# A two-block sequence model on one core: the recurrence's elementwise part moved from its eight units of 128 tokens into the projections, by pairs of heads and halves of the tokens

## The chip, the cores and the metric

The kernel runs as one program on one core of a Trainium2 chip. The metric is the device time of one execution in microseconds (us), the median of several runs. The engines are called PE (TensorE, matrix products), DVE (VectorE), ACT (ScalarE), POOL (GpSimd) and SP (SyncE, which here only issues DMAs). Each engine takes its own instructions in a fixed order and waits for the others by semaphores.

## The reference

Two blocks over 1024 tokens (16 more in the first) of width 1024, in float32. The first block (a state-space branch, an mLSTM branch and a gated FFN) is not touched. The second block normalizes, projects, and runs two mixers side by side: an 8-head recurrence (RWKV-7, 64 wide) and an 8-head dilated attention. An output product and an FFN follow. The part that the change moves is the recurrence:

```python
def _rwkv7_scan(r, decay, k, v, kk, a):
    def step(state, inp):
        r_t, w_t, k_t, v_t, kk_t, a_t = inp
        sa = jnp.einsum('bhvk,bhk->bhv', state, -kk_t)
        state = (state * w_t[:, :, None, :]
                 + sa[..., None] * (kk_t * a_t)[:, :, None, :]
                 + v_t[..., None] * k_t[:, :, None, :])
        return state, jnp.einsum('bhvk,bhk->bhv', state, r_t)
...
    p = p + (_token_shift(p) - p) * shift_mix
    w_log = -jax.nn.softplus(-(w0 + jnp.tanh(wd) @ w_lora_up)) - 0.5
    decay = jnp.exp(-jnp.exp(w_log.astype(f32)))
    a = jax.nn.sigmoid(a0 + ad @ a_lora_up)
    kk = heads(k * k_k)
    kk = kk / jnp.maximum(jnp.sqrt(jnp.sum(kk * kk, axis=-1, keepdims=True)), 1e-12)
    k = k * (1.0 + (a - 1.0) * k_a)
...
    bonus = jnp.sum(rh * kh * r_k.astype(f32), axis=-1, keepdims=True) * vh
```

The kernel computes the scan in chunks of 32 tokens: in a chunk a triangular system is solved, which turns the 32 steps into small matrices; a chain of products then carries the state from chunk to chunk.

## The kernel before

A scheduler with a model of the engines lays out each engine's instructions when the program is built, so the order on an engine is fixed, and an instruction whose input is late holds up all that stand behind it on that engine. Tiles live in pools by tag, with a number of buffers each: `W` 6, `V` 4, `A` and `L` 3, `J`, `B`, `K` 2, and `U`, which holds the matrix `M` of the triangular system, 1.

Around the change the second block runs these stages:

- **`rkv`** (L1333): twelve projections by `shifted` (L1297), for k, then r, then v, four groups of 128 columns each. A group is 48 products of 128x512 (three per 128 rows of the input, for float32 accuracy), in two halves of 512 tokens; here a **chunk** is one half, 24 products. DVE copies a half out (`p<-pm,rs`), POOL takes the difference of neighbouring tokens (`d`), DVE mixes. ACT and DVE split each weight tile into a high and a low part (`whi`, `wlo`). Groups of k go through `removal` (L1354: scaling, norm over a head). All results go to DRAM (`drkv`).
- **`rwkv`** (L1532): eight units u0 to u7 of 128 tokens. `rwkv_unit` (L1373) loads four tiles of 128x4x128 (partitions x head pairs x tokens) from `drkv`, through ACT's DMA queue, computes the decay by small products (`pa<-sl,lw`, L1390), tanh, a running sum (L1395) and exponentials, then about twenty elementwise operations. The operands go to `products` (L1429), whose first result is masked into `MM`. `MM` goes to DRAM (`dm`) and comes back as `M`, arranged for POOL. The **solve** is 31 steps of two POOL instructions (`fs<-Z,M`, `Z<-Z,fs`). Its result goes to DRAM (`dz`) and comes back as `xt`. All of these transfers go through SP.
- **`rwkv_maps`** (L1470) makes four 96x96 maps per head from `xt`, one unit later, and **`rwkv_chain`** (L1515) carries the state through them, two units later.
- **`attn_in`** (L1617): 24 chunks of projections for the attention, whose products the scheduler lays between those of the recurrence.
- The attention itself, whose products are ordered by hand; its first comes after the last products of the recurrence's chain.

`M` has one buffer, so a unit's `M` is loaded only when the solve before has ended.

Of the kernel before, what the change touches and what calls it, by code (L numbers as in the profile page):

```python
# [48 lines left out]
class Build:  # L49
# [1211 lines left out]
    def lora_weights(self):  # L1261

        self.reset = self.small([P, P], tag="reset", bufs=1)
        self.nc.gpsimd.memset(self.reset, 1.0)
        self.nc.gpsimd.memset(self.reset[:, 0:P:32], 0.0)
# [53 lines left out]
    def lora_part(self, part):  # L1319

        nc = self.nc
        raw = self.small([64, NT], tag="lrw", bufs=1)
        self.dma(out=raw, in_=self.dlora[:64, NT * part:NT * part + NT])
        sl = self.small([96, 2, NT], F32R, tag="sl", bufs=1)
# [8 lines left out]
    def rkv(self):  # L1333
# [4 lines left out]
        for i in (1, 0, 2):  # L1338
            for j in range(4):
# [6 lines left out]
                for h in range(2):  # L1346
                    ps = self.bank([P, 4, P], "c1")
                    for k in range(4):
                        self.nc.tensor.transpose(ps[:, k], t[:, 512 * h + 128 * k:512 * h + 128 * k + 128], self.ident)
                    vn = t[:, 512 * h:512 * h + 512].rearrange("p (k v) -> p k v", v=P)  # L1350
                    self.nc.scalar.copy(vn, ps)
                    self.dma(out=self.dvn[512 * h:512 * h + 512, j].rearrange("(k t) v -> t k v", t=P), in_=vn)

# [19 lines left out]
    def rwkv_unit(self, u, sl):  # L1373

        nc, v, pool, par = self.nc, self.nc.vector, self.nc.gpsimd, self.par
        t0 = P * u
        ch = lambda t: t.rearrange("p q (c t) -> p q c t", t=32)
        tw, ta, kk = (self.slot([P, 4, P], name="pr", tag="W") for _ in range(3))
        cs, rn, K, V = (self.slot([P, 4, P], name="pr", tag="V") for _ in range(4))
        R = self.slot([P, 4, P], name="R", tag="K")  # L1380
        wd = self.small([64, 4, 4, 2], tag="wd", bufs=4)
        cols = lambda n: [(par[n] if isinstance(n, str) else n)[:, q:q + 1] for q in range(4)]
        for i, t in ((3, kk), (0, R), (1, K), (2, V)):
            self.store(out=t, in_=self.drkv[i, :, :, t0:t0 + P].rearrange("q p t -> p q t"))

        own = slice(P * (u % 2), P * (u % 2) + P)
        for q in range(4):
            ps = self.bank([P, 2, NT], "a")
            for i in range(2):
                nc.tensor.matmul(ps[:, i], self.lw[:, i, q * P:q * P + P], sl[:, i], start=True, stop=True)  # L1390
            self.act(tw[:, q], ps[:, 0, own], AF.Tanh, scale=0.5, bias=self.w0h[:, q:q + 1])
            self.act(ta[:, q], ps[:, 1, own], AF.Tanh, scale=0.5, bias=self.a0h[:, q:q + 1])
        self.ts(tw, tw, 1.0, ALU.add)
        for q in range(4):
            v.tensor_tensor_scan(out=cs[:, q], data0=self.reset, data1=tw[:, q], initial=0.0, op0=ALU.mult, op1=ALU.add)  # L1395
        rate = -0.5 * math.exp(-0.5)
        W, WI = tw, cs
        self.act(tw, cs, AF.Exp, scale=rate)
        self.act(cs, cs, AF.Exp, scale=-rate)
        for e in range(2):  # L1400
            v.tensor_copy(wd[:, :, :, e], ch(W)[64 * e:64 * e + 64, :, :, 31])

        for q, (a, b) in enumerate(zip(cols(self.ka1), cols(self.ka0))):
            self.ts(rn[:, q], ta[:, q], a, ALU.mult, b, ALU.add)
        self.stt(ta, ta, 1.0, kk, ALU.add, ALU.mult)
        self.tt(ta, ta, WI, ALU.mult)
        self.tt(ch(kk)[:, :, :, 1:], ch(kk)[:, :, :, 1:], ch(W)[:, :, :, :31], ALU.mult)
# [761 lines left out]
```

## Time and profile before

| | |
|---|---|
| time, median of 3 runs | 3239.7 us (3235.3 to 3243.54) |
| profiled execution | 3233.1 us, its span 3231.4 us |
| busy in the span | PE 3009.3 us (93%), DVE 2009.6 (62%), POOL 1335.0 (41%), ACT 1142.4 (35%) |
| chain that ended last | PE 61%, DVE 11%, POOL 7%, issue 5%, DMA 4% |
| moved by DMA | 336.83 MB, mean 104 GB/s |

The span runs from the first to the last instruction of the profiled execution. The chain is followed back from the end, at each step to what released the instruction. Shares of a whole span average over stages with different limits, so the rows further down are cut to stages: `rkv` from 1642.7 to 1796.5 us, the eight solves from 1831.9 to 2150.0 us, the last products of the chain at about 2194 us.

### The profile page before, as it was taken

How to read it: one execution, taken by the hardware profiler on the slowest of the kernel's cores; microseconds unless marked ns; L12 is line 12 of the kernel's file. 1: busy time of each engine (PE TensorE's matmuls, PEld its weight loads, DVE VectorE, ACT ScalarE, POOL GpSimd, SP SyncE). 2: the span in 40 equal slices, each digit the busy share in tenths (PEclk: the TensorE clock that was granted, in tenths of full speed). 3: DMA queues.
4: the chain of work that ended last, by engine and by line, in shares of the span. 5: the costliest groups of instructions: out<-in, count | busy, mean ns of one | idle time of the engine just before them, and what ended most of it. 6: DMA issues, size and time to landing. Idle time of an engine off the chain costs nothing.

```text
span 3231.4 us, 52682 instructions
## 1 busy us (share of the span) xinstructions
PE 3009.3 (93%) x20614; PEld 2678.5 (83%) x20614; DVE 2009.6 (62%) x3618; ACT 1142.4 (35%) x2168; POOL 1335.0 (41%) x1291
## 2 busy tenths in 40 slices
PE   7999999989799999999999988788988899999998
PEld 6999998979799999877877776677778788887777
DVE  7556654674676666466776555558656766664666
ACT  3344313334343333311333323424444333334111
POOL 3767310033654444232532365543214744454430
PEclk9999999989799999999899989858998899999999
DMA  5333532335222222432223554533425122224321
GB/s 148 86 94 111 174 98 59 105 101 139 78 66 79 81 82 81 150 104 74 90 95 131 146 126 112 137 99 108 115 98 196 53 85 79 80 83 174 113 85 53
DMA packets 322535, 336.83 MB, mean 104 GB/s; under 512 B 60081, under 2 KB 270734, under 8 KB 322286
## 3 DMA queue, kind: packets, MB, share of 16 engines
q1 hardware_dynamic: 289646, 310.38, 31.0%
q10 hardware_dynamic: 32640, 23.08, 2.3%
q8 instruction: 162, 2.65, 0.3%
q14 instruction: 87, 0.71, 0.1%
HBM read 232.66 MB, written 96.40 MB: 102 GB/s over the span
## 4 chain that ended last, share of the span: by engine, by line
PE 61%; DVE 11%; POOL 7%; issue 5%; DMA 4%; ACT 2%; SPq 2%; ACTq 0%; DVEq 0%; POOLq 0%
PE pm L196 13%; PE pm L197 12%; PE pm L198 12%; PE px L197 5%; PE px L196 5%; PE px L198 5%; POOL fs L149 2%; POOL Z L149 2%; DVE dn L149 2%; SPq L142 2%; PE px L292 1%; DVE t L149 1%; PE pa L1877 1%; DMA M<-dm 1%; PE pc L1604 1%
## 5 line engine op out<-in xcount | busy, mean ns | idle before, releaser
L196 PE MATMUL pm<-xh,whi 128*128 128x512 f32 (+5 forms) x1344 | 446.9, 333 | 14.2 <-DVE th L149 11.5
L198 PE MATMUL pm<-xh,wlo 128*128 128x512 f32 (+5 forms) x1344 | 446.8, 333 | 0.0
L197 PE MATMUL pm<-xl,whi 128*128 128x512 f32 (+5 forms) x1344 | 446.4, 332 | 0.0
L149 DVE TENSOR_TENSOR y<-y,pm 128x512 f32<-128x512 f32 (+1 forms) x336 | 218.1, 659 | 159.4 <-PE pm L198 159.1
L196 PE MATMUL pm<-dn,dn 128*128 128x512 f32 (+1 forms) x736 | 286.0, 389 | 6.5 <-DVE y L149 6.2
L196 PEld LDWEIGHTS pm<-xh,whi 128*128 128x128 f32 (+1 forms) x1344 | 257.8, 192 | 35.8 <-DVE th L149 12.4
L197 PE MATMUL pm<-dn,dn 128*128 128x512 f32 (+1 forms) x736 | 282.4, 384 | 1.3 <-POOL dn L149 1.3
L198 PE MATMUL pm<-dn,dn 128*128 128x512 f32 (+1 forms) x736 | 282.5, 384 | 0.0
L197 PEld LDWEIGHTS pm<-xl,whi 128*128 128x128 f32 (+1 forms) x1344 | 257.6, 192 | 19.7 <-issue 0.9
L198 PEld LDWEIGHTS pm<-xh,wlo 128*128 128x128 f32 (+1 forms) x1344 | 257.8, 192 | 19.1 <-issue 0.5
L149 POOL TENSOR_TENSOR dn<-hid,dn 128x1024 fp32r<-128x1024 f32 x44 | 131.8, 3012 | 250.9 <-ACT dn L1161 250.9
L197 PE MATMUL px<-t,sh 128*128 128x258 f32 (+2 forms) x684 | 218.7, 320 | 6.9 <-DVE t L149 6.8
L196 PE MATMUL px<-t,sh 128*128 128x258 f32 (+2 forms) x684 | 217.2, 318 | 0.4 <-DVE gt L149 0.3
L198 PE MATMUL px<-t,sl 128*128 128x258 f32 (+2 forms) x684 | 216.1, 316 | 0.0
L149 DVE TENSOR_TENSOR wlo<-wraw,whi 128x1024 fp32r<-128x1024 f32 (+2 forms) x114 | 153.9, 1351 | 76.2 <-ACT whi L170 74.7
L196 PEld LDWEIGHTS pm<-dn,dn 128*128 128x128 f32 x736 | 138.2, 188 | 43.7 <-DVE y L149 14.2
L170 ACT CAST whi<-wraw 128x1024 fp32r<-128x1024 f32 (+2 forms) x114 | 103.4, 908 | 185.7 <-PE pm L197 154.8
L197 PEld LDWEIGHTS pm<-dn,dn 128*128 128x128 f32 x736 | 138.4, 188 | 29.9 <-POOL dn L149 1.7
L198 PEld LDWEIGHTS pm<-dn,dn 128*128 128x128 f32 x736 | 138.2, 188 | 30.0
L170 ACT CAST dn<-wd 128x1024 fp32r<-128x1024 f32 x44 | 46.1, 1048 | 290.8 <-PE pm L197 290.3
L197 PEld LDWEIGHTS px<-t,sh 128*128 128x128 f32 x684 | 131.3, 192 | 17.9 <-DVE t L149 9.1
L149 POOL TENSOR_TENSOR wraw<-wraw,par 128x1024 f32<-128x1024 f32 (+1 forms) x36 | 73.4, 2041 | 169.0 <-DMA wraw<-in_w_in_dram 128.7
(600 smaller groups left out, 8788.6 us busy)
## 6 DMA issues: line engine op xcount, KB each, us to landing
wraw<-in_w_in_dram SPq DMA_DIRECT2D x61, 512.0 KB
dhid<-up SPq DMA_DIRECT2D x44, 512.0 KB
wd<-in_w_ffn_down_dram SPq DMA_DIRECT2D x44, 512.0 KB
hid<-dhid SPq DMA_DIRECT2D x44, 512.0 KB
wra<-in_w_ffn_up_dram SPq DMA_DIRECT2D x33, 512.0 KB
wrb<-in_w_ffn_up_dram SPq DMA_DIRECT2D x33, 512.0 KB
dg<-th SPq DMA_DIRECT2D x16, 514.0 KB
wraw<-in_w_out_dram SPq DMA_DIRECT2D x16, 512.0 KB
```

The source lines that it names most:

```text
L142: self.nc.sync.dma_start(out=out, in_=in_)
L149: (eng or self.nc.vector).tensor_tensor(out=o, in0=a, in1=b, op=op)
L170: self.nc.scalar.copy(hi, src)
L196: nc.tensor.matmul(ps, a[0], b[0], start=start, stop=False, **kw)
L197: nc.tensor.matmul(ps, a[0], b[1], start=False, stop=False, **kw)
L198: nc.tensor.matmul(ps, a[1], b[0], start=False, stop=stop, **kw)
L292: self.nc.tensor.matmul(ps[:bw, i:i + 1], src[:, i * bw:i * bw + bw], self.ones[:, 0:1], start=start and i == 0, stop=stop and i == n - 1)
L1604: nc.tensor.matmul(ps, w[:, k], (yh, yl, yh)[q][:, a:b], start=i == 0, stop=i == 11)
L1877: nc.tensor.matmul(self.po[:, i - 4 * ch], pT[:, i * P - a:i * P - a + P], self.vx[j % 2][:, k].rearrange("p e v -> p (e v)")[:, 2 * e:2 * ...
```

## The change

The elementwise part of `rwkv_unit` becomes a function of its own, `prepare(q, half)`, called eight times from `rkv`: for each pair of heads q (one group of 128 columns) and each half of 512 tokens, on tiles of 128x512. `rkv` now takes k, v and r of one group in turn, then that group's two `prepare`s. A `prepare` loads its four tiles from `drkv`, and stores four results to a new DRAM tensor `dprep` and the bonus to `dbon`, all through SP. A unit then only loads its four tiles from `dprep`, through SP, and starts with `products`. It needs one half's `prepare` of all four pairs, so u0 needs that of the last pair. The transposed copy of v gets a buffer of its own (`B`) instead of overwriting its source. `MM` gets its own buffer in `W`. One tile holds the decays at the ends of all chunks (`wd`).

Instructions, before to after: decay products 64 of 256 columns to 16 of 512; tanh 64 of 128x128 to 16 of 128x512; running sums, scalings by `k_a` and multiplications by `r_k` each 32 of 128x128 to 8 of 128x512; 40 DMA issues leave ACT (32 loads, 8 stores of the bonus); SP gets 32 loads of `drkv`, 32 stores and 32 loads of `dprep` and 8 stores of the bonus (256 KB each). POOL's instructions stay the same in number.

```diff
     def rkv(self):
...
-        for i in (1, 0, 2):
-            for j in range(4):
+        self.dprep = self.dram([4, 4, P, T2], "dprep")
+        self.wd = self.small([64, 4, 32, 2], tag="wd", bufs=1)
+        sl = [self.lora_part(h) for h in range(2)]
+        for j in range(4):
+            for i in (1, 2, 0):
                 t = self.shifted(512 * i + j * P, P, self.par["mix"][:, 4 * i + j:4 * i + j + 1])
                 self.dma(out=self.drkv[i, j], in_=t)
...
-                    vn = t[:, 512 * h:512 * h + 512].rearrange("p (k v) -> p k v", v=P)
+                    vn = self.slot([P, 4, P], name="vn", tag="B")
...
+            for h in range(2):
+                self.prepare(j, h, sl[h])
+
+    def prepare(self, q, half, sl):
+        nc, v, par = self.nc, self.nc.vector, self.par
+        a, b = CH2[half]
+        ch = lambda t: t.rearrange("p (c t) -> p c t", t=32)
+        tw, ta, kk = (self.slot([P, 512], name="pr", tag="W") for _ in range(3))
+        cs, rn, K, V = (self.slot([P, 512], name="pr", tag="V") for _ in range(4))
+        R = self.slot([P, 512], name="pr", tag="K")
+        for i, t in ((3, kk), (1, K), (0, R), (2, V)):
+            self.dma(out=t, in_=self.drkv[i, q, :, a:b])
+        col = lambda n: (par[n] if isinstance(n, str) else n)[:, q:q + 1]
+        for i, (t, bias) in enumerate(((tw, self.w0h), (ta, self.a0h))):
+            ps = self.q_ps([P, 512])
+            nc.tensor.matmul(ps, self.lw[:, i, q * P:q * P + P], sl[:, i], start=True, stop=True)
+            self.act(t, ps, AF.Tanh, scale=0.5, bias=col(bias))
+        self.ts(tw, tw, 1.0, ALU.add)
+        v.tensor_tensor_scan(out=cs, data0=self.reset, data1=tw, initial=0.0, op0=ALU.mult, op1=ALU.add)
...
+        self.stt(rn, R, col("r_k"), K, ALU.mult, ALU.mult)
+        self.tt(R, R, W, ALU.mult)
+        self.tt(K, K, WI, ALU.mult)
+        for i, t in enumerate((ta, kk, R, K)):
+            self.dma(out=self.dprep[i, q, :, a:b], in_=t)
+        ps = self.q_ps([P, 512])
+        nc.tensor.matmul(ps, self.blk, rn, start=True, stop=True)
+        self.tt(rn, ps, V, ALU.mult)
+        self.dma(out=self.dbon[q, :, 0, a:b], in_=rn)
...
-    def rwkv_unit(self, u, sl):
+    def rwkv_unit(self, u):
+        nc, pool = self.nc, self.nc.gpsimd
         t0 = P * u
...
-        for i, t in ((3, kk), (0, R), (1, K), (2, V)):
-            self.store(out=t, in_=self.drkv[i, :, :, t0:t0 + P].rearrange("q p t -> p q t"))
...
+        ta, kk, MM = (self.slot([P, 4, P], name="pr", tag="W") for _ in range(3))
+        K, R = (self.slot([P, 4, P], name="pr", tag="V") for _ in range(2))
+        for i, t in enumerate((ta, kk, R, K)):
+            self.dma(out=t, in_=self.dprep[i, :, :, t0:t0 + P].rearrange("q p t -> p q t"))
```

The new order of instructions on three engines, at the places that matter:

**PE, the first products of u0.** Before, counted from the last product of `rkv`, they stand behind 3.67 chunks of `attn_in` (`pm` are the projections, `pq` with 32x32 the products of u0, `pa` its decay products for the next pair of heads):

```order
L196 MATMUL pm_2944_21502<-xh_16171,whi_21471 128x512
L197 MATMUL pm_2944_21502<-xl_16172,whi_21471 128x512
L198 MATMUL pm_2944_21502<-xh_16171,wlo_21472 128x512
L1429 MATMUL pq_2309_17679<-pr_17623,pr_17622 32x32 x16
L1429 MATMUL pq_2310_17697<-pr_17623,pr_17622 32x32 x16
L1390 MATMUL pa_17978<-sl_17614,lw_16410 128x256 x2
L196 MATMUL pm_2944_21502<-xh_16184,whi_21471 128x512
L197 MATMUL pm_2944_21502<-xl_16185,whi_21471 128x512
```

After, the first of the two stands behind 6.46 chunks, around the bonus product (`blk`) of the last `prepare`:

```order
L196 MATMUL pm_2977_21500<-xh_16156,whi_21495 128x512
L197 MATMUL pm_2977_21500<-xl_16157,whi_21495 128x512
L1443 MATMUL pq_2401_17971<-pr_17961,pr_17960 32x32 x7
L1397 MATMUL pq_2392_17954<-pr_17922,blk_16386 128x512
L1443 MATMUL pq_2401_17971<-pr_17961,pr_17960 32x32 x9
L198 MATMUL pm_2977_21500<-xh_16156,wlo_21496 128x512
L196 MATMUL pm_2977_21500<-xh_16171,whi_21495 128x512
```

and the second behind 7.33:

```order
L198 MATMUL pm_2978_21526<-xh_16128,wlo_21496 128x512
L196 MATMUL pm_2978_21526<-xh_16143,whi_21495 128x512
L197 MATMUL pm_2978_21526<-xl_16144,whi_21495 128x512
L1443 MATMUL pq_2402_17989<-pr_17961,pr_17960 32x32 x16
L1450 MATMUL pq_2404_18012<-ident_66,pr_17960 128x128 x4
L198 MATMUL pm_2978_21526<-xh_16143,wlo_21496 128x512
```

Before, the two stood next to each other (they are those of the two halves of the partitions, and `MM` needs both); now the second is 3.67 chunks later than it was. The products of the maps move in the same way: those of u0 stand behind 12.17 chunks (8.33 before), and u4's behind all 24 (20.4 before).

**SP, between the solves of u2 and u3.** Before, `dz` is the store of u2's solve, `xt` its way back, `dm` and `M` are those of u3:

```order
L142 DMA dz_18709<-Z_18610 256x1x32 x4
L142 DMA dqkv_21408<-at_21752 128x1024
L142 DMA wraw_22023<-in_w_in_dram 128x8x128
L142 DMA xt_17610<-dz_18709 32x8x32 x3
L142 DMA dm_18947<-pr_18853 32x8x32 x4
L142 DMA ST_19214<-dvn_16713 32x512
L142 DMA xt_17610<-dz_18709 32x8x32
L142 DMA M_19078<-dm_18947 32x1024 x4
```

After, the same transfers (`dz_18886` of u2, `dm_19077` and `M_19204` of u3), now with loads from `dprep` for a later unit among them:

```order
L142 DMA dz_18886<-Z_18787 256x1x32 x4
L142 DMA ro_21830<-dqkv_21312 16x8x128
L142 DMA ro_21831<-dqkv_21312 8x8x128
L142 DMA xt_17958<-dz_18886 32x8x32 x4
L142 DMA pr_19449<-dprep_16714 128x4x128
L142 DMA pr_19450<-dprep_16714 128x4x128
L142 DMA dm_19077<-pr_19032 32x8x32 x4
L142 DMA ro_21831<-dqkv_21312 8x8x128
L142 DMA ro_21830<-dqkv_21312 16x8x128
L142 DMA M_19204<-dm_19077 32x1024 x4
```

The order of `dz`, `xt`, `dm`, `M` stays; two loads of 128x4x128 stand between `xt` and `dm`, and loads for the attention (`ro`) are there instead of a weight load.

**DVE, in `rkv`, around the second `prepare` of the first pair.** `p` copies a chunk out of PE's result, `wlo` is a weight's low part, `rm` belongs to `removal`; `pr` are the tiles of `prepare`:

```order
L156 SCALAR_TENSOR_TENSOR d_17182<-d_17182,par_117,p_17128 128x1024
L156 SCALAR_TENSOR_TENSOR pr_16961<-pr_16961,pr_16962 128x512
L149 TENSOR_TENSOR pr_16965<-pr_16965,pr_16964 128x512
L1383 COPY wd_16715<-pr_16960 64x16 x2
L153 TENSOR_SCALAR rm_17106<-pc_2248_17112 128x512
L149 TENSOR_TENSOR pr_16961<-pr_16961,pr_16963 128x512
L149 TENSOR_TENSOR pr_16962<-pr_16962,pr_16960 128x16x31
L156 SCALAR_TENSOR_TENSOR pr_16964<-pr_16967,par_117,pr_16965 128x512
L149 TENSOR_TENSOR p_17208<-pm_2264_17209,rs_16111 128x512
L153 TENSOR_SCALAR pr_17000<-pr_17000 128x512
L149 TENSOR_TENSOR pr_16967<-pr_16967,pr_16960 128x512
L149 TENSOR_TENSOR pr_16965<-pr_16965,pr_16963 128x512
```

Before, no `pr` stood there: the operations of `prepare` now lie singly among those that release PE's buffers and make its weights. Three of the eight (the second half of pair 2, both of pair 3) have their products on PE behind the last chunk of `rkv`.

## Rows read from the trace of the kernel before

**Rows 1.** Chain of waits from the end of `rkv` to the attention, by line.

```profile
by line: POOL fs L149 19.2%; POOL Z L149 18.5%; issue 10.4%; SPq L142 9.6%; DMA M<-dm 6.1%; PE pc L1524 4.2%; DMA yn<-dyn 3.9%; PE pm L198 2.4%; PE pm L197 2.3%; PE pm L196 2.3%; DMA dz<-Z 2.2%; DMA dm<-pr 1.6%; PE pq L1429 1.3%; POOL ro L1
```

**Rows 2.** Busy time by stretch (us, busy and count by engine, clock, DMA).

```profile
core 0: us, PE busy (x) PEld busy (x) DVE busy (x) ACT busy (x) POOL busy (x), PEclk, DMA share, GB/s
1642.70:1796.50 153.80, 150.13 (x649) 118.67 (x648) 98.00 (x105) 50.37 (x60) 43.82 (x16) 1.00 0.39 127
1796.50:1831.90 35.40, 35.40 (x408) 28.76 (x410) 21.33 (x40) 13.66 (x32) 1.93 (x2) 1.00 0.60 162
2091.00:2150.00 59.00, 42.70 (x487) 37.71 (x488) 30.44 (x82) 14.54 (x28) 37.93 (x106) 0.58 0.38 103
```

**Rows 3.** Stretches of five solves, solve instructions alone; the sum is over all eight.

```profile
1831.86:1857.63 25.77, 20.99 (x62) 0.93 0.41 114
1867.45:1893.14 25.69, 20.91 (x62) 0.93 0.51 109
1899.83:1930.21 30.38, 23.42 (x62) 0.67 0.49 128
...
1989.29:2016.85 27.56, 22.78 (x62) 1.00 0.45 108
...
2122.47:2150.02 27.55, 18.04 (x62) 0.50 0.24 78
sum 221.87, POOL 167.55; mean POOL 20.94
```

**Rows 4.** SP's timeline between the solves of u3 and u4.

```profile
1972.33 2.55 SPq L142 DMA_DIRECT2D dz<-Z  x4
...
1979.25 1.93 SPq L142 DMA_DIRECT2D dm<-pr  x4
...
1982.41 2.42 SPq L142 DMA_DIRECT2D M<-dm  x4
```

**Rows 5.** POOL's timeline, first step of u4's solve.

```profile
1989.29 0.24 POOL L149 TENSOR_TENSOR fs<-Z,M 128x31 f32<-128x31 f32 x1 [10.93 <-DMA M<-dm]
```

**Rows 6.** DVE by line and form, `rkv` to u0's solve: count, busy us, mean ns.

```profile
L149 DVE TENSOR_TENSOR wlo<-wraw,whi 128x1024 fp32r<-128x1024 f32 x15 | 30.4, 2026 | 3.1 <-ACT whi L170 3.1
L149 DVE TENSOR_TENSOR p<-pm,rs 128x512 f32<-128x512 f32 x24 | 16.4, 686 | 13.1 <-PE pm L198 13.0
...
L149 DVE TENSOR_TENSOR pr<-pr,pr 128x512 f32<-128x512 f32 x3 | 2.1, 687 | 0.0
...
L1395 DVE TENSOR_TENSOR_SCAN pr<-reset,pr 128x128 f32<-128x128 f32 x4 | 1.4, 405 | 0.0
...
L153 DVE TENSOR_SCALAR pr<-pr,hw 128x128 f32<-128x128 f32 x4 | 1.1, 336 | 0.0
...
L156 DVE SCALAR_TENSOR_TENSOR pr<-pr,pr 128x512 f32<-128x512 f32 x1 | 0.7, 685 | 0.0
```

**Rows 7.** PE's timeline at u0's first products (start us, us, instruction, count).

```profile
1819.08 0.76 PE L1429 MATMUL pq<-pr,pr 64*32 64x32 f32 x64
1819.77 0.51 PE L1390 MATMUL pa<-sl,lw 96*128 96x256 f32 x2
1820.11 0.40 PE L196 MATMUL pm<-xh,whi 128*128 128x512 f32 x1
...
1823.36 0.39 PE L198 MATMUL pm<-xh,wlo 128*128 128x512 f32 x1
```

**Rows 8.** The bonus products by their source line (count, ns min/median/max, first and last start).

```profile
L1446 PE MATMUL pq<-pr,blk x16: 590/622/1167, 1829.1 to 2130.5; 128*128 128x512 f32 x16
```

**Rows 9.** POOL's timeline, two steps of u4's solve.

```profile
2007.12 0.29 POOL L149 TENSOR_TENSOR fs<-Z,M 128x54 f32<-128x54 f32 x1
...
2008.58 2.76 POOL L149 TENSOR_TENSOR fs<-Z,M 128x49 f32<-128x49 f32 x1
```

**Rows 10.** DVE's timeline in the same microseconds.

```profile
2008.78 1.21 DVE L149 TENSOR_TENSOR ro<-ro,rot 128x1024 f32<-128x1024 f32 x1
2009.91 0.68 DVE L149 TENSOR_TENSOR R<-R,pr 128x512 f32<-128x512 f32 x1
```

More of the change, by code (lines that the diff above doesn't have):

```diff
@@ L1261, in lora_weights @@
     def lora_weights(self):
-        self.reset = self.small([P, P], tag="reset", bufs=1)
+        self.reset = self.small([P, 512], tag="reset", bufs=1)
         self.nc.gpsimd.memset(self.reset, 1.0)
-        self.nc.gpsimd.memset(self.reset[:, 0:P:32], 0.0)
+        self.nc.gpsimd.memset(self.reset[:, 0:512:32], 0.0)
         lw = self.slot([96, 2, 512], F32R, "lw", "L")
@@ L1317, in lora_in, with lora_part @@
         self.dma(out=self.dlora[P:], in_=l2)
-    def lora_part(self, part):
+    def lora_part(self, half):
         nc = self.nc
-        raw = self.small([64, NT], tag="lrw", bufs=1)
-        self.dma(out=raw, in_=self.dlora[:64, NT * part:NT * part + NT])
-        sl = self.small([96, 2, NT], F32R, tag="sl", bufs=1)
+        raw = self.slot([64, 512], name="lrw", tag="V")
+        self.dma(out=raw, in_=self.dlora[:64, 512 * half:512 * half + 512])
+        sl = self.slot([96, 2, 512], F32R, "sl", "J")
         nc.scalar.copy(sl[:32, 0], raw[:32])
@@ new lines, in prepare @@
+    def prepare(self, q, half, sl):
[14 more added lines that the diff above has]
+        v.tensor_tensor_scan(out=cs, data0=self.reset, data1=tw, initial=0.0, op0=ALU.mult, op1=ALU.add)
+        rate = -0.5 * math.exp(-0.5)
+        W, WI = tw, cs
+        self.act(tw, cs, AF.Exp, scale=rate)
+        self.act(cs, cs, AF.Exp, scale=-rate)
+        for e in range(2):
+            v.tensor_copy(self.wd[:, q, 16 * half:16 * half + 16, e], ch(W)[64 * e:64 * e + 64, :, 31])
+        self.ts(rn, ta, col(self.ka1), ALU.mult, col(self.ka0), ALU.add)
+        self.stt(ta, ta, 1.0, kk, ALU.add, ALU.mult)
+        self.tt(ta, ta, WI, ALU.mult)
+        self.tt(ch(kk)[:, :, 1:], ch(kk)[:, :, 1:], ch(W)[:, :, :31], ALU.mult)
+        self.tt(K, K, rn, ALU.mult)
+        self.stt(rn, R, col("r_k"), K, ALU.mult, ALU.mult)
[7 more added lines that the diff above has]
+        self.dma(out=self.dbon[q, :, 0, a:b], in_=rn)
@@ L1370, in removal @@
         self.dma(out=self.drkv[3, j], in_=kk)
-    def rwkv_unit(self, u, sl):
-        nc, v, pool, par = self.nc, self.nc.vector, self.nc.gpsimd, self.par
+    def rwkv_unit(self, u):
+        nc, pool = self.nc, self.nc.gpsimd
         t0 = P * u
[L1377 to L1382, printed above, removed]
-        for i, t in ((3, kk), (0, R), (1, K), (2, V)):
-            self.store(out=t, in_=self.drkv[i, :, :, t0:t0 + P].rearrange("q p t -> p q t"))
[L1386 to L1407, printed above, removed]
-        self.tt(K, K, rn, ALU.mult)
-        for q, col in enumerate(cols("r_k")):
-            self.stt(rn[:, q], R[:, q], col, K[:, q], ALU.mult, ALU.mult)
-        self.tt(R, R, W, ALU.mult)
-        self.tt(K, K, WI, ALU.mult)
@@ L1444, in rwkv_unit @@
         by_tokens(kk, LR[:, :, 0, :64])
-        ps = self.q_ps([P, 4, P])
-        nc.tensor.matmul(ps, self.blk, rn, start=True, stop=True)
-        self.tt(rn, ps, V, ALU.mult)
-        self.store(out=self.dbon[:, :, 0, t0:t0 + P].rearrange("q p t -> p q t"), in_=rn)
         products((ta, R, LR[:, :, 1, 64:], 1), (kk, K, LR[:, :, 0, 64:], 0), (K, R, KT[:, :, 64:], 1))
@@ L1498, in rwkv_maps @@
                     self.tt(two[:, i, 4 * k:4 * k + 4], two[:, i, 4 * k:4 * k + 4], ps, ALU.add)
-        return maps, wd
+        return maps
     def map_ps(self, shape):
@@ L1513, in rwkv_state, with rwkv_chain @@
         return st.get(c)
-    def rwkv_chain(self, u, maps, wd):
+    def rwkv_chain(self, u, maps):
         nc = self.nc
```

16 lines of the change are left out of this document (7 added, 9 removed).

## Prediction, made before the changed kernel was run

> **What bounds the kernel now.** I read the shares of the whole span first and set them aside: a PE that is 93% busy on average says nothing of the stage that the change touches. The chain of waits from the end of `rkv` to the attention comes next [rows 1]: its two largest entries are the two POOL instructions of the solve, 19.2% and 18.5%, while each product line of PE has under 5%. So behind `rkv` the recurrence is a chain on POOL, and the projections of the attention are filler beside it. The stretches say the same of the two stages [rows 2]: in `rkv` PE is busy 150.1 of 153.8 us at full clock, DVE 98.0 and POOL 43.8, so PE bounds `rkv`; between 2091 and 2150 us, where the filler has run out, PE is busy 42.7 of 59 us at a granted clock of 0.58, and nothing waits for it for long.
>
> The rest is the solves [rows 3]. The eight run from 1831.86 to 2150.02 us, 318.2 us, of which 221.9 are solves, so the seven pauses between them sum to 96.3 us. A pause is a way through DRAM: SP issues the store of u3's result, `dz`, from 1972.33, only at 1979.25 `dm` of u4, and `M` at 1982.41; u4's first step starts at 1989.29, after 10.93 us of idle time put down to `M` [rows 4, 5]. SP works in order, so `dm` stands behind `dz`, though its data may be ready long before. Where `dm` was sent earlier, the pause is short: 6.7 us between u1 and u2, from 1893.14 to 1899.83 [rows 3].
>
> Everything is therefore one line: `rkv`, the way to u0's solve (1796.5 to 1831.86, 35.4 us), eight solves with pauses, the last maps and chain. What lengthens this line lengthens the kernel.
>
> **The change part by part.** *DVE in `rkv`.* One `prepare` is nine operations of 128x512 with two inputs at 0.69 us, 6.2 us; two scalings between 0.34 (a quarter of the columns) and 0.69, I take 0.43; two small copies, at most 0.34 each; and one running sum [rows 6]. No row shows a sum over 512 columns: from below it is one operation of that size, 0.69, from above four of 128 columns, 1.6; I take 1.2. That makes 8.5 us (7.9 to 9.2), 68 for eight. Five lie inside `rkv`, 43 us: DVE goes from 98 to about 141 us there. It still fits beside PE on average, but the first group has no `prepare`, so the last three groups are close to full, and the `pr` stand in front of `p<-pm` (which frees PE's buffers) and `wlo` (which makes its weights). From below these stalls cost nothing; from above, see the second rival. I take 12 us.
>
> *PE in `rkv`.* Thirteen decay products of 512 columns come in. Two of 256 take 0.34 us till the next product [rows 7], so 4.4 us, less what was in `rkv` before: I take 3.5. Five bonus products of two records each at 0.62 us [rows 8] are at most 1.24 us each, I take 1.1: 5.5. PE bounds this stage, so +9 us is on the path.
>
> *The way to u0's solve.* Before, u0's products stand behind 3.67 chunks of `attn_in` and run at 1819.08, 22.6 us behind the last copy of `rkv`. Fourteen products start in 3.25 us (1820.11 to 1823.36), 0.232 us each, so a chunk of 24 is 5.57 us [rows 7]: 3.67 chunks are 20.4 us of those 22.6. After, the second product, which `MM` needs, stands behind 7.33 chunks, 40.8 us, and behind the decay and bonus products of three `prepare`s, some 4: 45 us. That is +22 us, and it can't be less, since PE takes them in order. It can be more: u0's inputs now need the last group's r to go out to `drkv` and back, a `prepare` on a DVE that also serves the filler, and then `dprep` out and back. A load of `M` takes 4.5 us from the end of its issue to the first step [rows 4, 5]; two more such ways are 9 us. Inside the 45 us they are hidden if DVE is not late; if it is late, they are not. `dm` and `M` of u0 also share SP with loads for the next units (four issues take 1.9 us [rows 4]). For both I take +4 (0 to +13). The Trainium skill (DMA: Bandwidth & Descriptors, section Anatomy of one DMA — SWDGE (gpsimd) path) puts about 2.0 us of fixed cost on a DMA, most of it until the write is confirmed; it speaks against a way through DRAM. The transfers here are issued by SP, so no run shows its case exactly; by it the two ways would be an estimated 4 us, by the row 9, and the sum is the same by both as long as they are hidden.
>
> *The solves.* A step that takes 0.29 us takes 2.76 when DVE runs operations with two inputs from SBUF beside it (`ro` 1.21, `R` 0.68) [rows 9, 10]. `R<-R,pr` is one of a unit's elementwise operations, and these leave the stretch of the solves. Without them a solve is u7's: 18.04 us busy, against 20.9 to 23.4 for the four others shown [rows 3]. Six solves (u0 to u5) at 2 to 3.7 us are 12 to 22 us; the filler's own operations (`ro`, `wlo`) stay, so I take -16. The Trainium skill (SBUF — State Buffer, section SBUF: two separate sides) says that such a DVE operation and a GpSimd operation that reads SBUF lock each other out for a whole instruction, the first to start keeping the ports. The rows agree on the lock and not on who wins: the step was recorded 0.2 us earlier and yet waited. On the sum this has no effect.
>
> *The pauses.* The order on SP is what sets them, and it keeps `dz`, `xt`, `dm`, `M` for u3 to u5, now with two loads between `xt` and `dm`. Counting the rows in front of each `M` I get 8, 7, 17.5, 19, 16.5, 13 and 13 us, 94 in place of 96: -3 (from -15 to +8). What is gained is that `dm` is ready; what is late next is its place behind `dz`.
>
> *Hidden or equal.* The 40 DMA issues and 48 tanh instructions that ACT is rid of gain nothing, since no wait of the line above is for ACT, and its part of `prepare` costs nothing in `rkv`, where it was busy 50 of 153.8 us [rows 2]. 64 more transfers of 256 KB are 16.8 MB; DMA's share there was 0.39, so they fit, if the weight loads that SP now issues behind `dprep` stores come in time. The maps and the chain of the last unit stay as they are: 0, give or take 5.
>
> Sum: 9 + 12 + 22 + 4 - 16 - 3 = +28 us. On the profiled execution's 3233.1 us this is 3261; the median lies 6.6 us above it, so 3268.
>
> **The rivals.**
> *Short pauses (faster).* If `dm` leaves before `dz` for all units, since nothing precedes it any more but `products`, every pause is that between u1 and u2, 6.7 us: seven are 47, so -49 in place of -3. Then the time is 3268 - 46 = 3222. The point at which it decides is the sum of the pauses: under about 70 us the gain beats what `rkv` and u0 lose. For it: the short pause exists. Against it: SP's order is fixed, and for u3, u4, u5 and u6 `dm` stands behind `dz`. Chance 0.12.
>
> *DVE and POOL full in `rkv` (slower still).* If DVE's operations and POOL's exclude each other there too, the stage is no shorter than the sum: 98 + 43 + 43.8 = 185 us, 31 over the 153.8, in place of 9 + 12 = 21. For it: `wlo` takes 2.03 us on average there [rows 6], against 1.21 for an operation of that size in [rows 10]. That is some 12 us of lockout that the 98 already holds, so the true sum is a little smaller; but weights held up behind `dprep` stores on SP would add to it. Time 3278, up to 3300. Chance 0.25. The Trainium skill (SBUF — State Buffer, section Who interferes with whom) leads to the same case: by its rule of one side fully blocked, the sum of both engines is what such a stage lasts.
>
> *It cancels (no change).* `prepare` fits into DVE's gaps without a stall (0 for 12), u0's inputs are in time (0 for 4), solves gain the full 22, pauses 10: 9 + 22 - 22 - 10 = -1, 3239. For it: DVE waits for PE in front of `p` 13.1 us in `rkv`, so there are gaps [rows 6]. Against it: all of this has to come together. Chance 0.18.
>
> **How the numbers follow.** The forecast has 0.45, with its own range from 3250 to 3285. 0.3% (10 us) is about what a measurement of this kernel can tell from no change. Faster is the first rival and a little of the third's lower side, 0.14; within 0.3% the rest of it and the forecast's lower edge, 0.19; slower 0.67. The range leaves out most of the first rival and the far end of the second: 3234 to 3302.
>
> **What would show it.** In the profile after: `rkv` from its first to its last copy about 175 us (150 to 160 means that no stall came; 185 or more the second rival); u0's first solve step 58 to 66 us behind the last copy, where 35.4 stood; solves of u0 to u5 some 23 us, each step alike; pauses that sum to about 94 us (the first rival: about 50); PE's clock at half earlier, since the filler runs out before u4's maps. The prediction is wrong if u0's solve comes less than 50 us behind the last copy, or if the pauses shrink by more than 25 us.

## The result, and the profile after

The changed kernel takes 3259.94 us (median of 4 runs, 3257.14 to 3261.51) where the kernel before takes 3237.5 in the same comparison: 1.0065 times as long, with an interval from 1.0048 to 1.0083, or 22 us more. The forecast was 3268 us. Its profiled execution has a span of 3259.8 us, 28.4 more than before.

The stretches of the new kernel (columns as in [rows 2]): `rkv` from the last copy ahead of it to its own last copy, the way to u0's solve, and the stretch behind the last solve.

```profile
1646.50:1823.70 177.20, 165.53 (x694) 126.90 (x692) 141.03 (x181) 68.47 (x87) 43.61 (x16) 0.98 0.54 177
1823.70:1884.00 60.30, 55.10 (x462) 42.10 (x463) 35.98 (x56) 17.78 (x33) 2.37 (x2) 0.94 0.76 240
2172.00:2226.00 54.00, 42.70 (x267) 39.48 (x268) 34.00 (x111) 16.14 (x32) 11.87 (x15) 0.53 0.33 98
```

`rkv` takes 177.2 us for 153.8 [rows 2]. DVE is busy 141.0 us there for 98.0, as forecast, but not as worked out: `prepare`'s tiles (`pr`) are 53.4 us of it, not 43, and DVE's other work fell by about as much, to 87.6. PE is busy 165.5 for 150.1 and idle 11.7 for 3.7. Two lines of what PE waited for in this stretch (us in total, times, longest) name most of the idle time: a bonus product waits for DVE's `pr`, and the projections for DVE's copies of their bank.

```profile
PE pq L1397 <- DVE pr L156: 5.3, 2, 4.9
PE pm L196 <- DVE p L149: 3.2, 2, 2.6
```

Two groups of DVE's operations in `prepare`, up to u0's solve (count, busy us, mean ns):

```profile
L1377 DVE TENSOR_TENSOR_SCAN pr<-reset,pr 128x512 f32<-128x512 f32 x8 | 11.5, 1434 | 1.0 <-DMA dprep<-pr 0.9
...
L153 DVE TENSOR_SCALAR pr<-pr,hw 128x512 f32<-128x512 f32 x8 | 4.3, 542 | 11.1 <-DMA dbon<-pr 10.2 <-ACT pr L159 1.0
```

The running sum over 512 columns takes 1.43 us, between the 0.69 and 1.6 of the prediction. In front of the second group DVE stood idle for 10.2 us in all, because the store of a bonus (`dbon`) has to land before its tile can be used again.

From the last copy of `rkv` to u0's solve are 60.3 us in place of 35.4. What this way hangs on, from the second half of the products that `MM` needs to the loads of `M`, on PE, DVE and SP:

```profile
1868.37 0.46 PE L1443 MATMUL pq<-pr,pr 64*32 64x32 f32 x32
...
1868.90 0.29 DVE L149 TENSOR_TENSOR pr<-pq,mk 128x128 f32<-128x128 f32 x1 [1.58 <-PE pq L1443]
...
1868.53 5.73 SPq L142 DMA_DIRECT2D pr<-dprep  x4
1874.36 3.21 SPq L142 DMA_DIRECT2D dm<-pr  x4
1878.91 2.88 SPq L142 DMA_DIRECT2D M<-dm  x4
```

The second half of these products starts 44.7 us behind the last copy (22.6 before). PE is busy for 41.8 of the 44.7 us, so what it waits for on the way is little: the products stand behind others in its fixed order. `MM` is ready at 1869.2, but SP issues `dm` only at 1874.36, behind four loads from `dprep`; before, `dm` followed at once. The first step comes 15.5 us behind the products, 12.8 before.

Beside this way the last r goes out and back, and u0's other operands come in. Three pieces of the chain of waits in this stretch (start, us, what), which ends at PE's last product in it and not at the solve:

```profile
1833.16 6.88 DMA drkv<-d
...
1840.06 5.73 DMA pr<-drkv
...
1868.53 6.21 DMA pr<-dprep
```

The solves (solve instructions alone, as in [rows 3]):

```profile
1883.91:1911.59 27.68, 19.09 (x62) 0.80 0.72 167
1918.63:1942.54 23.91, 19.13 (x62) 1.00 0.48 126
1950.72:1973.85 23.13, 18.35 (x62) 0.85 0.59 160
...
2033.18:2057.78 24.60, 17.41 (x62) 1.00 0.35 105
...
2149.86:2172.27 22.41, 17.63 (x62) 0.58 0.17 48
sum 200.93, POOL 146.74; mean POOL 18.34
```

They last 200.9 us in sum for 221.9, and POOL is busy 146.7 for 167.6. From the start of the first to the end of the last, 1883.91 to 2172.27, are 288.4 us, so the pauses are 87.4 for 96.3. SP's timeline between the solves of u3 and u4 answers to [rows 4]:

```profile
2016.18 2.56 SPq L142 DMA_DIRECT2D dz<-Z  x4
...
2020.20 1.83 SPq L142 DMA_DIRECT2D xt<-dz  x4
...
2025.17 2.37 SPq L142 DMA_DIRECT2D dm<-pr  x4
2029.03 1.71 SPq L142 DMA_DIRECT2D M<-dm  x4
```

The order is the same as before, `dz`, `xt`, `dm`, `M`, and so is the pause: 2016.15 to 2033.18, 17.0 us. But here `dm` does not wait for its place on SP. Its data become ready on DVE at 2025.15, and SP issues it at 2025.17:

```profile
2024.67 0.48 DVE L149 TENSOR_TENSOR pr<-pq,mk 128x128 f32<-128x128 f32 x2
```

The products for it had ended on PE at 2015.9; DVE's operations in front of the mask waited for a load of the recurrence's output (`yn`). In the kernel before, `MM` of u4 was ready 11.5 us ahead of `dm`. Of the other late ones in the changed kernel, `MM` of u3 is ready 9.3 us ahead of its `dm`, and those of u5 to u7 2.5 to 4.0 us.

Behind the last solve the first product of u7's maps starts 17.4 us after the solve's end (9.0 before), and the last chain product ends at 2225.7, 53.4 us behind the solve (44.3 before).

```profile
2175.39 1.12 PE L1788 MATMUL pq<-ident,vT 128*128 128x128 f32 x4 [7.05 <-DMA vT<-dqkv]
...
2189.71 1.97 PE L1489 MATMUL pm<-LR,xt 128*128 128x96 f32 x8
```

PE's idle time behind the solve is 11.3 us for 3.3, and 7.0 of it are one wait: a transposition for the attention stands in front of the chain's products, and its load (`vT`) was issued only at 2172.0: `vT` has the one buffer of `M` (tag `U`), which the last solve reads until then. Before, that load also came at the end of the last solve, but PE did not wait for it.

So the balance of the profiled executions is: `rkv` +23.4, way to u0 +24.9, solves -20.9, pauses -8.9, behind the last solve +9.1, together +27.6; the stages ahead of `rkv` are 3.8 longer and those behind the recurrence 3.0 shorter, which gives the +28.4.

### The profile page after: what moved, and what is told of

It is laid out like the page before. It is cut to its first block, busy times and chain, and to the rows that moved or that the text cites. A ratio compares the mean times of both kernels' runs of the same rounds, so it can differ in the third digit from the quotient of the medians.

```text
span 3259.8 us, 52547 instructions
## 1 busy us (share of the span) xinstructions
PE 3021.2 (93%) x20566; PEld 2690.7 (83%) x20566; DVE 1996.4 (61%) x3542; ACT 1132.5 (35%) x2112; POOL 1319.5 (40%) x1291
## 5 line engine op out<-in xcount | busy, mean ns | idle before, releaser
L196 PEld LDWEIGHTS pm<-xh,whi 128*128 128x128 f32 (+1 forms) x1344 | 259.1, 193 | 43.3 <-DVE th L149 12.0
```

The costliest lines, as they stand in the source:

```text
L196: nc.tensor.matmul(ps, a[0], b[0], start=start, stop=False, **kw)
```

## The experiments

Each was timed against the kernel before on the same chip; its medians there lie between 3237.5 and 3241.6 us. Times of stages come from one profiled execution of each; that of experiment 4 lies 9 us above its median, that of 6 lies 9 below, those of 2 and 7 lie 5 and 6 above, the others within 4.

**1 and 2. What shortened the solves.** Extra DVE work in each unit of the changed kernel, ahead of its first products:

```diff
+        scr = MM[:, 2:]
+        for _ in range(20):
+            self.tt(scr, ta[:, 2:], kk[:, 2:], ALU.mult)
```

> The changed kernel, in which every unit gets 20 extra DVE operations of 128x256 with two SBUF inputs (their result is thrown away), about 8.4 us per unit, which is what a unit had before. If the solves became shorter because such operations no longer lie beside them (my theory), the POOL busy time of the solves goes from 146.8 us back to 158 to 168 us and the time from 3260 to 3270-3285. Rival (they became shorter for another reason: other filler beside them, a later place in the program): the busy time stays within 4 us of 146.8 and the time within 8 us of 3260.

and, instead of it, with one input:

```diff
+        scr = MM[:, 2, :4]
+        for _ in range(10):
+            nc.vector.tensor_reduce(out=scr, in_=ta, axis=AX.X, op=ALU.add)
```

> The same place in every unit, but 10 DVE sums over 128x512 with a single SBUF input, some 6 us per unit. If it is the second SBUF input that holds POOL up, the solves' busy time stays at 147 (+-4) us and the time at 3260 (+-8). Rival (any DVE work beside a solve slows it): 155 us or more, as in the experiment with two inputs.

Measured: 3274.2 us (1.0102, 1.0087 to 1.0117) with two inputs, 3260.6 us (1.0064, 1.0047 to 1.0081) with one. The solve of u1 and the sum, with two inputs:

```profile
1921.85:1946.92 25.07, 20.29 (x62) 1.00 0.40 100
...
sum 214.38, POOL 156.61; mean POOL 19.58
```

and with one:

```profile
1922.38:1945.47 23.09, 18.31 (x62) 1.00 0.47 127
...
sum 199.11, POOL 143.38; mean POOL 17.92
```

Two inputs bring back 9.9 of the 20.8 us of POOL's busy time, a little under what was expected, and 13.5 us of the solves' length; one input brings back nothing (143.4). From 1880 us on the extra operations are 55.5 us of DVE time with two inputs and 43.5 us with one, and inside the solves DVE's operations on `pr` are 39.3 us with two inputs and 27.8 with one, so the quantity alone does not tell them apart. It is the operations with two inputs from SBUF that hold POOL up, and their absence that shortens the solves. That only about half came back fits: inside the solves the kernel before has 67.5 us of DVE time on `pr` and the changed one 1.7, so the experiment put back 37.6 of 65.8.

**3. What DVE costs in `rkv` and on the way to u0.** Most of `prepare`'s arithmetic left out:

```diff
-        self.ts(rn, ta, col(self.ka1), ALU.mult, col(self.ka0), ALU.add)
-        self.stt(ta, ta, 1.0, kk, ALU.add, ALU.mult)
...
-        self.tt(K, K, WI, ALU.mult)
```

> The changed kernel with prepare cut: one scaling and seven of the nine two-input operations are left out (the products then take unscaled operands), some 5.3 us of 8.5 us each on DVE; its loads, stores, matmuls, tanh, running sum and exponentials stay. If DVE in rkv is the cause of 12 to 14 of the 23 us that rkv grew by, rkv from its first to its last copy comes down from 177 to 162-168 us, and u0's solve starts 50 to 57 us behind the last copy (60.2 now); time 3235-3247. Rival A (PE's extra products and waits for weights behind the stores on SP make up the 23): rkv stays at 174 or more. Rival B (u0's way is PE's order and DRAM alone): its 60 us stay within 3.

Measured: 3248.4 us (1.0017, 1.0005 to 1.0029). Its stretches (columns as above), `rkv` and the way to u0:

```profile
1647.50:1816.00 168.50, 162.01 (x677) 125.02 (x676) 111.36 (x138) 69.44 (x87) 42.58 (x16) 0.98 0.61 199
1816.00:1861.70 45.70, 44.43 (x442) 35.37 (x440) 20.50 (x32) 16.47 (x31) 2.86 (x2) 1.00 0.80 249
```

`rkv` falls by 8.7 us to 168.5, half a microsecond short of what was expected, and u0's way by 14.6 to 45.7, more than expected; the time misses its range by 1.4 us. DVE's work lengthens both. On u0's way it does so through the order: the products for `MM` start 28.5 us behind the last copy in place of 44.7, because the scheduler has laid them out earlier. (`prepare` has eight operations with two inputs, not the nine of the prediction; seven are left out here.) About 15 us of `rkv`'s growth stay without it, of which PE's busy time is 11.9; the rest was not separated.

**4. The order of the projections alone.** In the kernel before:

```diff
-        for i in (1, 0, 2):
-            for j in range(4):
+        for j in range(4):
+            for i in (1, 2, 0):
```

> The kernel before with one thing changed: rkv takes k, v, r of one group of columns in turn instead of all k, all r, all v; nothing else moves. My theory has no price for the order itself: rkv stays at 154 (+-3) us and the time within 6 us of 3238. Rival (the order costs, because the heavy groups of k with their norms are spread and the last group's products follow late): rkv grows by 8 us or more, and the time with it.

Measured: 3249.0 us (1.0032, 1.0016 to 1.0047). `rkv` and the way to u0:

```profile
1652.00:1805.50 153.50, 152.50 (x664) 121.03 (x663) 96.59 (x103) 50.07 (x58) 40.87 (x15) 1.00 0.38 121
1805.50:1853.00 47.50, 47.08 (x458) 37.96 (x457) 26.93 (x45) 12.74 (x29) 5.46 (x3) 1.00 0.59 168
```

`rkv` stays as it was (153.5), but u0's way is 47.5 us, 12 more than before: the last group's k and its norm now come just ahead of the end, where all of k had been ready long before. PE is busy for 47.1 of the 47.5 us: it works on the attention's projections, behind which the scheduler has put u0's products (they start 33.5 us behind the last copy, 22.6 before). Neither theory had this: the order costs, but behind `rkv`. Put beside experiment 3, it makes about 12 of the 25 us of u0's way the price of the order and about 13 to 15 that of `prepare` on DVE; that the two simply add was not tried.

**5. A second buffer for `M`.**

```diff
-        M = self.slot([P, 32, 32], name="M", tag="U")
+        M = self.M2 if u % 2 else self.slot([P, 32, 32], name="M", tag="U")
```

> The changed kernel with a second buffer for M (odd units use one in a slot that is free behind rkv); the order dz, xt, dm, M on SP stays for u3 to u7. If the pauses hang on dm's place behind dz (my theory), they stay near 87 us in sum (75 to 90; only those of u1 and u2 shrink) and the time is 3250-3262. Rival (they hang on M's single buffer, which has to wait for the end of the solve): under 50 us, time 3215-3225.

Measured: 3261.0 us (1.0072, 1.005 to 1.0095). The first five solves:

```profile
1879.93:1903.04 23.11, 18.41 (x63) 1.00 0.61 148
1903.00:1932.95 29.95, 18.97 (x64) 0.77 0.64 159
1932.91:1958.14 25.23, 18.45 (x63) 1.00 0.39 112
1974.36:1996.60 22.24, 17.46 (x62) 0.89 0.42 94
2022.34:2045.66 23.32, 18.54 (x62) 1.00 0.51 150
```

The pauses in front of u1 and u2, whose `dm` stands before the `dz` of the unit ahead, are gone (u0's solve ends at 1903.04, u1's starts at 1903.00). That in front of u4, where `dm` stands behind `dz` and `xt`, is 25.7 us. The sum is 84.5 for 87.4, as expected, and the single buffer is not what sets most of it. Where `dm` goes out before the solve ahead ends, the pause is `M`'s single buffer; where it goes out later, a second buffer does not help. That is not always SP's order: `MM` of u4 is ready at 2012.4, 15.8 us behind the solve's end, and `dm` goes out at 2012.5; DVE had stood still for 20.1 us, until a load of the attention (`ro`) came, with the masks of `MM` behind it. For u3, u5 and u6 `MM` was ready 8.8 to 15.5 us ahead of `dm`.

**6. First products a unit ahead.** The loads, first products, `dm` and `M` of unit u+1 are written ahead of the rest of unit u, with the second `M`:

```diff
-                cur = self.rwkv_unit(u)
+                head, nxt = nxt, self.unit_head(u + 1) if u + 1 < NU else None
+                cur = self.rwkv_unit(u, head)
```

> As the experiment with a second M, and the first products, dm and M of each unit are now written in the program ahead of the rest of the unit before (loads, products for MM, dm, M of unit u+1, then the other products of u). dm then stands before dz for u2 and u3, and M of u4 too; for u5 to u7 dm stands right behind dz and before xt. My theory: the pauses of the first units go to 1-3 us, the later ones to about 9, sum 25-50 in place of 87; time 3215-3235. Rival (the solves are no longer what the end waits for: maps and chain run behind them): the pauses shrink, the stretch from the last solve to the last chain product grows from 53 by nearly as much, time 3245 or more.

Measured: 3247.3 us (1.0021, 1.0005 to 1.0037). Solves u3, u4 and u5:

```profile
1960.86:1986.23 25.37, 18.80 (x64) 0.98 0.49 131
1986.18:2016.41 30.23, 19.83 (x63) 0.66 0.48 102
2029.07:2052.20 23.13, 18.35 (x62) 1.00 0.56 132
```

The first four pauses are gone and the sum is 44.2 for 87.4, as expected. But the time falls by 13 us, not by 43, and misses the expected range: the solves are 13.4 us longer in sum (214.3), with work of the attention on POOL between their steps, and the last chain product ends 64.7 us behind the last solve, 11.3 more. With 43.3 us less in the pauses and 2.7 on u0's way this makes 21 us less, and the profiled execution is 23 us shorter than that of the changed kernel.

**7 and 8. Half of the `prepare`s behind u0**, in the changed kernel and in that of experiment 6:

```diff
-            for h in range(2):
+            for h in range(1 if j else 2):
                 self.prepare(j, h, sl[h])
...
                 cur = self.rwkv_unit(u)
+                if u == 0:
+                    for q in range(1, 4):
+                        self.prepare(q, 1, self.sl[1], late=True)
```

> The changed kernel, but of the second half's prepares only the first pair's stays in rkv; those of pairs 1 to 3 are written behind unit u0 (units u4 to u7 need them). If rkv and u0's way lengthen because DVE is full, rkv falls from 170 to 160-167 us (first to last copy of its 24), u0's solve starts 35 to 48 us behind the last copy (60 now), solves of u0 to u2 take 4 to 10 us more in sum, time 3230-3245. Rival (u0's way is the transfers through DRAM, which stay): it remains above 52 us, time 3250 or more.

> Both of the two experiments before together. If their terms are on one path they add: about 57 to 65 us less than the changed kernel, 3190-3205. Rival (with the solves that early, maps and chain at half clock behind them set the end): 3215 or more, with a stretch from the last solve to the last chain product above 75 us.

Measured: 3272.6 us (1.011, 1.0088 to 1.0133) and 3257.8 us (1.0058, 1.0036 to 1.008). In the first of the two:

```profile
1852.73:1884.22 31.49, 26.72 (x62) 0.56 0.49 159
1910.59:1933.84 23.25, 18.47 (x62) 1.00 0.39 108
```

u0's solve comes 39.4 us behind the last copy and `rkv` is 11 us shorter, as expected, and yet the time is 13 us longer than the changed kernel's, where 15 to 30 less were expected: u0's solve now holds 26.7 us of busy time, the pause in front of u1 is 26.4 us, and the stretch behind the recurrence is 1053 us for 1034: what was moved out of one place waits in the next. In the second, the last solve ends at 2104.4, 68 us sooner than in the changed kernel, and the last chain product at 2212.1, 14 us sooner: 107.7 us behind it. The rival's marks were met, but not by its reason: the granted clock is 0.76 and 0.95 between 2104 and 2176 us, and the attention's projections, which end at 2070 in the changed kernel, are copied out until 2176.1; u7's maps start 72 us behind the last solve.

**9. The kernel before, with first products a unit ahead**, a second `M` and a second set of the unit's tiles:

```diff
+                head, nxt = nxt, None
+                if u + 1 < NU:
+                    nxt = self.unit_head(u + 1, sl)
+                cur = self.rwkv_unit(u, head)
```

> The kernel before, not the changed one, with each unit's loads, elementwise part, first products, dm and M written ahead of the rest of the unit before it, a second M and a second set of the unit's tiles (both in slots that are free behind rkv). rkv and u0's way stay as before (154 and 35 us, +-4). My theory: the pauses shrink from 96 to 40-55 us without the price in rkv; the solves stay at 215-225 us, since the elementwise operations still lie beside them; the stretch from the last solve to the last chain product grows from 44 to 55-70; time 3205-3228, faster than both kernels. Rival (maps and chain take all of it back): 3235-3245.

Measured: 3327.0 us (1.0261, 1.0243 to 1.0278); both theories missed. The recurrence ends at 2172.4, 22 us sooner than before, but the copies of the attention's projections (duration ns min/median/max, first and last start) are these:

```profile
L149 DVE TENSOR_TENSOR at<-pm,rs x24: 672/691/692, 2096.8 to 2250.8; 128x512 f32<-128x512 f32 x24
```

The first starts at 2096.8 us, which in the kernel before is at 1803.0: the new order puts PE's filler behind the last solve, which ends at 2097.1, instead of beside the solves, and the attention waits for it. The pauses are 71.9 us in sum, where 40 to 55 were expected.

**10. r taken directly.** `prepare` reads r from the projection's own tile:

```diff
-        R = self.slot([P, 512], name="pr", tag="K")
-        for i, t in ((3, kk), (1, K), (0, R), (2, V)):
+        R = r[:, a:b]
+        for i, t in ((3, kk), (1, K), (2, V)):
```

> The changed kernel, in which prepare takes r from the tile that the projection has just made instead of through drkv (in the last group r is the last to come). The chain of waits of the changed kernel has 6.9 us for that store and 5.7 for the load. If u0's way hangs on this transfer, u0's solve starts 47 to 53 us behind the last copy (60.3 now) and the time is 3247-3254. Rival (the DVE work of the last prepares sets it, and the transfer is hidden beside the prepare before): 57 us or more, time within 5 us of 3260.

Measured: 3239.1 us (0.9996, 0.9986 to 1.0005): one load fewer per `prepare`, and the whole loss is gone, which neither expectation had. u0's way is 54.9 us, 5.4 less, between the two: `MM` is ready 2.1 us sooner behind the last copy, and `dm` waits 1.8 us on SP where it waited 5.2. The larger part is elsewhere: the pauses are 75.7 us, 11.7 less. SP's timeline between the solves of u2 and u3:

```profile
1968.17 0.32 SPq L142 DMA_DIRECT2D M<-dm  x1
1968.58 2.55 SPq L142 DMA_DIRECT2D dz<-Z  x4
1971.17 1.52 SPq L142 DMA_DIRECT2D M<-dm  x3
1972.92 1.80 SPq L142 DMA_DIRECT2D xt<-dz  x4
```

`dm` of u3 is no longer here: it went out at 1955.97, 0.9 us after `MM` was ready and long before the solve's end; those of u6 and u7 also start ahead of `dz`, and these pauses are 6.8, 10.1 and 8.7 us, where the changed kernel has 15.2, 12.7 and 12.5; for u4 and u5 it is still behind, with 16.3 and 18.5. The stretch behind the recurrence is 6.7 us shorter too. Why the new order has `MM` ready sooner, and why that last stretch is shorter, no run shows.

**11. Experiments 6 and 10 together.**

> The changed kernel with r taken directly, and with loads, first products, dm and M of each unit written ahead of the rest of the unit before, with a second M (the two experiments that made it faster, together). Alone they gave 21 and 13 us, the one with shorter pauses and u0's way, the other with the first four pauses gone. Both shorten pauses, so they can't add fully: my theory is 3222-3232, pauses 35-50, u0's solve 52-58 us behind the last copy, the stretch from the last solve to the last chain product 60-75; faster than both kernels. Rival (the end of the recurrence is held by maps and chain on PE, which what is gained in the pauses only makes wait): 3236-3246, chain end not earlier than the 2213 us of r taken directly alone.

Measured: 3248.4 us (1.0028, 1.0016 to 1.0041), slower than experiment 10 alone. The solve of u7, and the first product of u7's maps on PE:

```profile
2107.56:2130.21 22.65, 17.87 (x62) 0.73 0.11 34
```

```profile
2176.72 1.97 PE L1507 MATMUL pm<-LR,xt 128*128 128x96 f32 x8
```

The last solve ends at 2130.2, 27 us sooner than in experiment 10, but u7's maps start 46.5 us behind it, and the last chain product ends at 2211.2, where it was at 2213.0. Two lines of what PE waited for between 2003 and 2130 us:

```profile
PE pc L1552 <- ACT yv L1556: 13.8, 3, 12.3
PE pc L1552 <- DVE A L149: 11.7, 1, 11.7
```

They are of the chain: it waits for the maps of its own unit and for the copy of its last result. The rival was right in the main (its time was at most 3246, its chain end not before 2213): maps and chain set this end. What spaces them at some 35 us per unit was not separated further.

**12. r taken directly, and only the last `prepare` behind u0.**

> The changed kernel with r taken directly, and with only the last prepare (second half of the last pair, which u4 is the first to need) written behind unit u0; u0's first products then stand behind two chunks of attn_in in PE's order, not behind six to seven. If u0's way hangs on the DVE work of the last prepares and on PE's order behind it, u0's solve starts 40 to 48 us behind the last copy (54.9 with r direct alone, 60.3 in the changed kernel), the pause in front of u1 grows by no more than 8 us, and the time is 3225-3236, faster than both kernels. Rival (as with three late prepares: what u0 gains, u1 and the attention's projections lose): pause in front of u1 above 17 us or the stretch behind the recurrence longer than 1037 us, time 3239 or more.

Measured: 3252.4 us (1.0043, 1.0029 to 1.0056). The first two solves:

```profile
1863.65:1890.45 26.80, 22.02 (x62) 0.85 0.47 146
1899.53:1923.14 23.61, 18.83 (x62) 0.57 0.36 85
```

u0's solve comes 41.0 us behind the last copy and u1's pause is 9.1 us, both as expected, and yet the time is 13 us above experiment 10: the other pauses grow (96.3 in sum), the last chain product ends at 2210.4, and the stretch behind it is 1038.5 us, 11 longer. My theory missed here too; the rival's marks, this stretch above 1037 us and a time of 3239 us or more, were met.

No version beats the kernel before; experiment 10 equals it.

## Why the prediction was right

It forecast a slower kernel from terms on one line, and the terms are those that the profile shows. That the sum is so near is partly luck. It was +28 us, and the profiled executions differ by 28.4; the medians differ by only 22.4, because the profiled execution before lay 4.4 us below its median and the one after 1.6 us above. Inside the sum, solves and pauses gave 10.8 us more than forecast, and the last maps and chain took 9.1 where nothing was forecast.

- *PE in `rkv` +9, stalls +12.* Together 23.4 for 21. PE's idle time grew by 8.0 us and its busy time by 15.4. The thirteen decay products and ten bonus records came as counted; in the busy time are also 15 products of 128x512 beyond the 576 of the twelve projections, some 3.5 us, since PE was already at the attention's when DVE copied out the last chunk. Experiment 3 confirms that DVE is behind 8.7 us of it. DVE's 141 us were right by luck: the terms were 98 + 43, and 87.6 + 53.4 were measured. The count of nine operations with two inputs was wrong (eight), and several operations took longer than the rows had them. The second rival (185 us) did not come: 177.2.
- *Way to u0 +22 and +4.* +24.9, and here the mechanism was right in both parts. PE's order puts the second half of u0's first products 44.7 us behind the last copy (45 worked out, +22.1), and the rest of the way is 2.7 us longer, with `dm` behind loads on SP. That the 45 came so exactly is luck: PE had done one of the 7.33 chunks before that copy, so 6.33 lie behind it (35 us), and the products between them and the waits took some 9 us in place of 4. "It can't be less" held for the order as it was laid out; the order itself comes from the scheduler, and experiments 3 and 4 show what moves it: the order of the projections alone is 12 us, the DVE work of `prepare` about 13 to 15.
- *Solves -16.* -20.9 in length, -20.8 in busy time; experiments 1 and 2 show the cause, though they put back only part of it. The Trainium skill (SBUF — State Buffer, section Who interferes with whom) sets a DVE instruction with one SBUF input apart from one with two, and experiments 1 and 2 agree: 156.6 us of busy time against 143.4.
- *Pauses -3.* -8.9, inside the range. "The order on SP is what sets them" was only part of it. Over all fourteen profiles, a pause is 6.7 to 10.8 us where all of `dm` is issued before the solve ahead ends (0 to 2.3 with a second `M`). Where its issue starts after that end, the pause is 7 to 11 us more than the delay, 10.6 to 26.4 us (five straddle the end, with 8.7 to 13.2). But what delays `dm` is SP's order in some units and a late `MM` in others (u4: 0.0 us between the mask and `dm`). No run changes SP's order alone.
- *The first rival (short pauses make it faster)* was right to be put low: pauses of 44 us (experiment 6) gave 13 us, not 43. It was put low for another reason, though: the prediction held that the time follows the solves; experiments 6 and 11 show that maps and chain stand close behind.
- *Last maps and chain 0, give or take 5.* This step failed: +9.1. The prediction took the stretch behind the last solve as fixed and left out what stands in front of the chain in PE's order there. In the trace 7.0 us are the wait for `vT`. It is not shown that this wait is the cause: in experiment 5 PE does not wait for `vT`, and the stretch is 54.2 us all the same. The clock is not the cause: the granted clock is 0.53 in this stretch and was 0.50, near the lower of its two levels (1.2 GHz) in both. What is left is how far the units ahead have come: u6's chain ends 23 us behind the last solve, 18 before. That was not tested by itself.
- *It cancels (no change)* failed as a rival because `prepare` did not fit into DVE's gaps (23.4 us for its 9) and because it, too, had nothing for the last maps and chain. Experiment 10 is the nearest to it: no change, but by another way, with `rkv` still at 177 us.
- *The signs.* `rkv`, u0's way, the pauses and an earlier fall of PE's clock came as named (0.65 and 0.53 in the solves of u5 and u6, 1.00 and 0.74 before). Solves of "some 23 us, each step alike" did not: those of u0, u3 and u5 take 27.7, 27.1 and 28.8 us.

## What to carry to other kernels

Work that is moved from a stage that waits to one that PE bounds does not come free, even where the engine that does it is idle a third of the time: what counts is whose buffers it stands in front of, and what the first item of the next stage needs last. Before a move, ask for each stage which input comes last, since an order of loops that costs nothing in its own stage can delay the next one. Before a pause is put down to a queue's order, look when the data of its transfer were ready: here the same kind of pause came from the queue in one unit and from a late input in the next. And when a chain of waits gets shorter, look at the second longest: in experiment 11 the last solve ended 27 us sooner and the last chain product 2.

## What was not expected of the hardware

Transfers took longer than the row from which they were priced. On the way to u0's solve the DMA engines are busy 0.76 of the time, and the store of r takes 6.9 us, its load 5.7, the load of `dprep` 6.2; the prediction had put 4.5 us on such a way, from a load of `M` in a stretch with less traffic. The transfers also differ in size, and whether the traffic is the cause was not tried. u0's solve paid little for them: PE stood still for 2.8 us on the way to its products.
